# The order of the chosen-key attention, the recurrence's heads and two branches in a two-block layer on one core

## The chip, the core and the metric

The program runs on one core of a Trainium2 chip, in one launch. The metric is the device time of that core in microseconds (us). Three runs of the kernel before gave 1706.37 us as the median, from 1705.73 to 1706.66.

## What is computed

The program is a first block (a convolution branch, a gated linear attention, a hierarchical mixture of experts) and behind it a second block over the same T = 256 tokens of width 1024. The change lies in the second block alone. There u is the normed input and every token gets four branch outputs of width 256: the recurrence (index 0), a pool mixer (1), an attention over chosen keys (2) and an attention into 256 memory tokens (3). Cut to what matters:

```python
z = u @ w_in[l]
(hq, hf, hi, hg, pz, sq, sk, sv, iq, ik, iw, mq) = jnp.split(z, split_pts, axis=-1)
y_a = hgrn2_mixer(hq, hf, hi, hg, lb_all[l], hgrn_norm[l])
y_b = pool_mixer(pz, pool_w[l], pool_scale[l])
y_c = dsa_mixer(sq, sk, sv, iq, ik, iw)
y_m = mem_attention(mq, mk, mv)
merged = None
for bi, y in enumerate((y_a, y_b, y_c, y_m)):
    term = jax.nn.sigmoid(u @ w_gate[l, bi]) * (y @ w_branch[l, bi])
    merged = term if merged is None else merged + term
h = h + rms_norm(merged @ w_out[l], norm_mix_post[l])
u = rms_norm(h, norm_ffn_pre[l])
gt, up = jnp.split(u @ w_ffn_gate_up[l], 2, axis=-1)
h = h + rms_norm((jax.nn.silu(gt) * up) @ w_ffn_down[l], norm_ffn_post[l])
```

The sum over the branches may be taken in any order, so the four branches may follow each other in any order, as long as the weights come in the same one.

## The kernel before, in words

All matrices are fp32. A weight arrives by DMA on SP's queue in pieces of 128x2048 (1 MB, `Stream.load`, L139) and is split in two (`Split.weights`): a high half that ACT copies out (L170), and a low half, raw minus high, whose first 1280 columns DVE computes (L172) and whose other 768 POOL does (L173). Activations are split likewise by ACT and DVE (`Split.act`, L178 and L179; `yh`, `yl`, `uh`, `ul`, `mh`, `ml` are such halves). A product is three matmuls on PE (`Split.mm`, L186 to L188). High and low halves have three buffers each, PSUM's bank tag `ps` (the tiles `pst`) has four, the gates' `sg` two.

In the second block the work around the change is this. `recur(h)` (L1226) does one of the recurrence's four heads: exponentials, elementwise levels on DVE and POOL, matmuls with masked copies in between (L1262, L1263), states (L1268 to L1283). Every second head closes with a norm: square (L1289, ACT), a matmul that sums it (L1291), square root (L1293, ACT, with a load of the root's table), reciprocal and two products on DVE (L1294 to L1296), and a split of the result (L178, L179), of which branch 0's product needs both halves. `choose(t)` finds the top 64 keys for one tile of 128 tokens, `chosen(t)` the attention over them: four logits (L1384, PE), bias and scale (L1391) and the maximum (L1393, both DVE), exponentials (L1322, ACT, with its own table), reciprocals and scaling (L1323, L1324, DVE), four transposes (L1326, PE) copied by ACT (L1333), the values' matmuls (L1338), and a split of the output.

`branch(b)` takes one piece of branch weights and four pieces of gate weights: 4 x 48 gate matmuls of `u` and four groups of 12 matmuls of the branch's output. ACT takes the sigmoid of a gate (L1433), DVE multiplies it with the product (L1435 in the first branch, L1437 after), POOL adds it to `merged` (L1438). Behind the branches stand `w_out` (4 pieces, 96 matmuls over `mh`, `ml`), `add_normed` (the norm of its output, from L1470), `normed_split` (the norm ahead of the FFN: L1103, L1105, a diagonal matrix `dg` at L1109, a turned product at L1115, then `uh` and `ul`), and the FFN.

No engine's order is written out by hand here, except around the norm between `w_out` and the FFN, where ACT, DVE and POOL keep the order of the code. Elsewhere a list scheduler sets each engine's order from the order of the calls (L1445 to L1459) and from its own model of durations; then the engines run through those orders as they stand. Moving two calls can so move instructions anywhere between them and the next fixed point. The order of the weights in memory (`stream2`, L1693) has to be that of the calls.

Of the kernel before, what the change touches and what calls it, by code (L numbers as in the profile page):

```python
# [128 lines left out]
class Stream:  # L129
# [20 lines left out]
    def take(self):  # L150
        self.ahead(1)
        return self.ready.pop(0)
# [894 lines left out]
def second(tc, A, k, out):  # L1047
# [9 lines left out]
    def pt(shape=(P, 512)):  # L1057
        return k.ps.tile(list(shape), F32, tag="ps", name="pst", bufs=k.n_ps)

    def mx(shape=(P, 512)):  # L1060
        return k.ps.tile(list(shape), F32, tag="mx", name="mxt", bufs=8 - k.n_ps)

    with ExitStack() as es:
# [254 lines left out]
        def attend(h, lg, nk, scale, nm, pts):  # L1318

            pe = tp.tile([P, T], F32, tag="a1", name="pe", bufs=k.n_a1)  # L1320
            sm = tp.tile([P, 1], F32, name="sm", bufs=4)
            S.activation(pe[:, :nk], lg, AF.Exp, scale=scale, bias=nm, accum_out=sm[:])  # L1322
            V.reciprocal(sm[:], sm[:])  # L1323
            V.tensor_scalar(pe[:, :nk], pe[:, :nk], sm[:], None, op0=OP.mult)  # L1324
            for c in range(nk // P):
                nc.tensor.transpose(pts[c][:, h], pe[:, c * P:(c + 1) * P], ident)  # L1326

        def values(t, nk, pts, src, y):

            pT = []  # L1330
            for c in range(nk // P):
                pT.append(tp.tile([P, 4, P], F32, tag="a2", name="pT", bufs=k.n_a2))
                S.activation(pT[c][:], pts[c][:], AF.Copy)  # L1333
            py = mx((P, 2, P))
            for h in range(4):
                r = slice(64 * (h % 2), 64 * (h % 2) + 64)
                for c in range(nk // P):
                    nc.tensor.matmul(py[r, h // 2], src(c, h), pT[c][:, h], start=c == 0, stop=c == nk // P - 1)  # L1338
            s = slice(t * P, (t + 1) * P)
            sp.act(yh[y][:, :, s], yl[y][:, :, s], py[:])  # L1340
# [37 lines left out]
        def chosen(t):  # L1378
            nk, neg = P * (t + 1), negs[t]
            pl2 = [mx((P, 2, T)) for _ in range(2)]  # L1380
            for j in range(2):
                for i in range(2):
                    r = slice(64 * i, 64 * i + 64)
                    nc.tensor.matmul(pl2[i][:, j, :nk], sqT[r, j, t * P:(t + 1) * P], skT[r, :nk],  # L1384
                                     start=True, stop=True)
            pts = [mx((P, 4, P)) for _ in range(nk // P)]
            for i in range(2):
                lg = tp.tile([P, 2, T], F32, tag="a2", name="lg", bufs=k.n_a2)
                nm = tp.tile([P, 2], F32, name="nm")
                for j in range(2):  # L1390
                    V.scalar_tensor_tensor(lg[:, j, :nk], pl2[i][:, j, :nk], 64.0 ** -0.5, neg[:, :nk],  # L1391
                                           op0=OP.mult, op1=OP.add)
                V.tensor_reduce(nm[:], lg[:, :, :nk], axis=AX.X, op=OP.max, negate=True)  # L1393
                for j in range(2):
                    attend(2 * j + i, lg[:, j, :nk], nk, 1.0, nm[:, j:j + 1], pts)
            values(t, nk, pts, lambda c, h: sv[:, c], 2)
# [19 lines left out]
        def branch(b):  # L1416

            nonlocal merged
            first = merged is None
            if first:  # L1420
                merged = ap.tile([P, NB, T], F32, tag="merged", name="merged")
            bh, bl = sp.weights(take(), 2)
            for half in range(2):
                def gate_in(i, o):
                    if i % 2 == 0:
                        return
                    blk = half * 4 + i - 1
                    p = pt((P, 2, T))
                    for j in range(2):
                        s = slice((blk + j) * P, (blk + j + 1) * P)  # L1430
                        sp.mm(p[:, j], lambda c: (bh[:, c, s], bl[:, c, s]), lambda c: (yh[b][:, c], yl[b][:, c]), 2)
                    sg = tp.tile([P, 2, T], F32, name="sg", bufs=k.n_sg)
                    S.activation(sg[:], dn.banks[i // 2][:], AF.Sigmoid)  # L1433
                    if first:
                        V.tensor_tensor(merged[:, blk:blk + 2], sg[:], p[:], op=OP.mult)  # L1435
                    else:
                        V.tensor_tensor(sg[:], sg[:], p[:], op=OP.mult)  # L1437
                        G.tensor_tensor(merged[:, blk:blk + 2], merged[:, blk:blk + 2], sg[:], op=OP.add)  # L1438

                dn.turned(X, gate_in)  # L1440
# [4 lines left out]
        choose(1)  # L1445
        choose(0)
        recur(0)
        recur(1)
        recur(2)
        recur(3)  # L1450
        chosen(1)
        chosen(0)
        branch(1)
        branch(3)
        post = ap.tile([P, 2, D], F32, tag="ln2", name="post")
        nc.sync.dma_start(post[:], A["rows2"][:, 2 * D:4 * D].rearrange("o (a d) -> o a d", a=2)
                            .to_broadcast([P, 2, D]))
        branch(0)
        branch(2)  # L1459
        gain = ap.tile([P, D], F32, tag="gain", name="gain")  # L1460
        nc.sync.dma_start(gain[:], A["rows2"][:, 5 * D:].to_broadcast([P, D]))

        def add_normed(t, banks, gain, last=False):

            ss = tp.tile([P, 3], F32, name="rss", bufs=4)
            halves = [slice(0, 512), slice(512, 1024)]
            for half, s in enumerate(halves):
                o = banks[half][:]
                junk = tp.tile([P, 512], F32, tag="a2", name="junk", bufs=k.n_a2)
                S.activation(junk[:], o, AF.Square, accum_out=ss[:, half + 1:half + 2])  # L1470
                V.tensor_tensor(o, o, gain[:, s], op=OP.mult)
                yield
            rs = rms_scale(nc, k, ss)
            yield
            for half, s in enumerate(halves):
                o = banks[half][:]
                V.scalar_tensor_tensor(x[:, t, s] if last else o, o, rs, x[:, t, s], op0=OP.mult, op1=OP.add)
            yield
# [18 lines left out]
        with tc.manual_schedule(engines={E.Activation, E.DVE, E.Pool}):  # L1497
# [7 lines left out]
            a, b = [add_normed(t, banks[t], post[:, 0]) for t in range(2)]  # L1505
# [74 lines left out]
        a, b = [add_normed(t, banks[t], post[:, 1], True) for t in range(2)]  # L1580
# [8 lines left out]
def body(tc, A, out):  # L1589
# [6 lines left out]
    with ExitStack() as es:  # L1596
# [24 lines left out]
        with ExitStack() as mid:  # L1621
# [15 lines left out]
            experts(tc, A, k)  # L1637
        k.stream.open([A["s2"][i] for i in range(A["s2"].shape[0])])
        second(tc, A, k, out)


# [31 lines left out]
def stream2(f):  # L1673

    w, gate, br = f["w_in_2"][0], f["w_gate_2"][0], f["w_branch_2"][0]
    gu, dn = f["w_ffn_gate_up_2"][0], f["w_ffn_down_2"][0]
    out = []

    def add(m):
        out.extend(m.reshape(2, 4, P, 512).transpose(0, 2, 1, 3).reshape(2, P, PIECE))  # L1680

    def rows(m):

        out.append(m.reshape(2, P, D).transpose(1, 0, 2).reshape(P, PIECE))

    add(np.concatenate([w[:, 1536:1792], w[:, 1024:1280]], axis=1))
    add(w[:, 512:1024])
    add(np.concatenate([w[:, 2760:3016], w[:, 2688:2752], w[:, 2048:2112], w[:, 2752:2760], w[:, 2112:2176],
                        np.zeros((D, 56), np.float32)], axis=1))
    add(w[:, 2176:2688])  # L1690
    add(w[:, 0:512])
    add(np.concatenate([w[:, 1792:2048], w[:, 1280:1536]], axis=1))
    for b in (1, 3, 0, 2):  # L1693
        rows(br[b])
        for half in range(2):
            add(gate[b][:, half * 512:half * 512 + 512])
    for half in range(2):
        add(f["w_out_2"][0][:, half * 512:half * 512 + 512])
    for i in range(11):
        add(np.concatenate([gu[:, 256 * i:256 * i + 256], gu[:, D_FF + 256 * i:D_FF + 256 * i + 256]], axis=1))  # L1700
        if i:
            rows(dn[256 * i - 256:256 * i])
    rows(dn[2560:])
    m = f["w_mem_kv_2"][0].reshape(2, 4, P, 512).transpose(0, 2, 1, 3).reshape(2, P, PIECE)
    return np.stack(out), m


def layouts(inp):
# [40 lines left out]
    a["s1"], a["x_by8"] = stream1(f), by8(f["x"])  # L1749
    a["wflr"] = f["w_in"][0][:, 5120:5136].reshape(NB, P, 16).transpose(1, 0, 2)  # L1750
    a["s2"], a["wm"] = stream2(f)
    for n in ("w1", "w3", "w2", "mem_2"):
        a[n] = f[n]
# [17 lines left out]
```

## Time and profile before

| | |
|---|---|
| median of three runs | 1706.37 us |
| profiled execution | 1704.52 us |
| its span | 1702.7 us |
| mean granted TensorE clock | 0.956 |
| PE, DVE, ACT, POOL busy in the span | 88%, 32%, 28%, 28% |
| first block | to some 1225 us |
| recurrence, attentions, branches | to some 1480 us |
| w_out, norms, FFN | to the end |

All times in the trace are microseconds from the start of the span. PE's column tells how long matmuls ran, not how fast: the granted clock stands in a column of its own, and a slow stretch looks busy.

### The profile page before, as it was taken

How to read it: one execution, taken by the hardware profiler on the slowest of the kernel's cores; microseconds unless marked ns; L12 is line 12 of the kernel's file. 1: busy time of each engine (PE TensorE's matmuls, PEld its weight loads, DVE VectorE, ACT ScalarE, POOL GpSimd, SP SyncE). 2: the span in 40 equal slices, each digit the busy share in tenths (PEclk: the TensorE clock that was granted, in tenths of full speed). 3: DMA queues.
4: the chain of work that ended last, by engine and by line, in shares of the span. 5: the costliest groups of instructions: out<-in, count | busy, mean ns of one | idle time of the engine just before them, and what ended most of it. 6: DMA issues, size and time to landing. Idle time of an engine off the chain costs nothing.

```text
span 1702.7 us, 23642 instructions
## 1 busy us (share of the span) xinstructions
PE 1500.3 (88%) x9883; PEld 996.1 (59%) x9883; DVE 544.0 (32%) x1032; ACT 469.0 (28%) x640; POOL 484.9 (28%) x332
## 2 busy tenths in 40 slices
PE   8999999986898878787877878887799998999998
PEld 7999995332353323232322323332499997979997
DVE  5888685110200000010000000000464856453333
ACT  6435651101100000000000000000465544563433
POOL 6777832000000000000000000000354454556563
PEclk9999999997989999999998989999899999999999
DMA  7453679999999999999999999999744332534552
GB/s 276 156 180 140 232 308 349 421 425 426 426 426 426 427 426 426 426 426 426 426 426 426 426 427 426 426 426 426 317 174 149 123 125 100 186 144 178 186 185 74
DMA packets 75693, 533.19 MB, mean 313 GB/s; under 512 B 8497, under 2 KB 9009, under 8 KB 11970
## 3 DMA queue, kind: packets, MB, share of 16 engines
q1 hardware_dynamic: 74178, 526.61, 76.2%
q10 hardware_dynamic: 1408, 5.06, 0.8%
q8 instruction: 78, 1.28, 0.3%
q14 instruction: 29, 0.24, 0.0%
HBM read 530.59 MB, written 1.05 MB: 312 GB/s over the span
## 4 chain that ended last, share of the span: by engine, by line
DMA 45%; PE 26%; DVE 3%; ACT 1%; issue 0%; SPq 0%; DVEq 0%; ACTq 0%
DMA w<-in_w_dram 44%; PE pst L188 6%; PE pst L187 6%; PE pst L186 6%; PE mxt L187 2%; PE mxt L186 2%; PE mxt L188 2%; DMA w<-in_wm_dram 1%; PE pst L833 1%; ACT hi L170 1%; DVE lo L172 0%; PE mxt L1262 0%; PE pst L852 0%; PE pst L1115 0%; PE mxt L1231 0%
## 5 line engine op out<-in xcount | busy, mean ns | idle before, releaser
L173 POOL TENSOR_TENSOR lo<-w,hi 128x768 fp32r<-128x768 f32 (+2 forms) x112 | 381.0, 3407 | 354.7 <-ACT hi L170 244.8
L833 PE MATMUL pst<-w,xe 128*32 128x512 f32 x2048 | 351.2, 669 | 89.1 <-DMA w<-in_w_dram 88.1
L833 PEld LDWEIGHTS pst<-w,xe 128*32 128x32 f32 x2048 | 83.3, 120 | 333.2 <-DMA w<-in_w_dram 163.5
L170 ACT ACTIVATE hi<-w 128x2048 fp32r<-128x2048 f32 (+1 forms) x112 | 209.0, 1868 | 213.0 <-PE pst L187 119.0
L878 POOL TENSOR_TENSOR sw<-S,Wt 128x64 f32<-128x64 f32 x128 | 33.5, 294 | 802.2 <-DVE S L888 558.9
L187 PE MATMUL pst<-ul,hi 128*128 128x256 f32 x736 | 208.6, 284 | 0.0
L188 PE MATMUL pst<-uh,lo 128*128 128x256 f32 x736 | 208.0, 283 | 0.4 <-DVE lo L172 0.4
L186 PE MATMUL pst<-uh,hi 128*128 128x256 f32 x736 | 208.1, 283 | 0.0
L845 DVE TENSOR_TENSOR hd<-si,pst 128x128 f32<-128x128 f32 x64 | 18.5, 289 | 560.0 <-ACT si L844 560.0
L852 PE MATMUL pst<-w,hd 128*32 128x512 f32 x1024 | 171.3, 620 | 25.3 <-DVE hd L845 24.1
L172 DVE TENSOR_TENSOR lo<-w,hi 128x1280 fp32r<-128x1280 f32 (+1 forms) x77 | 124.2, 1613 | 152.4 <-ACT hi L170 142.5
L823 PEld LDWEIGHTS pst<-S,x 128*128 128x128 f32 x1024 | 126.1, 200 | 61.8 <-issue 61.7
L836 ACT ACTIVATE hs<-pst 128x512 f32<-128x512 f32 x32 | 19.1, 597 | 454.5 <-PE pst L833 454.5
L188 PEld LDWEIGHTS pst<-uh,lo 128*128 128x128 f32 x736 | 138.3, 188 | 2.4 <-DVE lo L172 0.9
L186 PEld LDWEIGHTS pst<-uh,hi 128*128 128x128 f32 x736 | 138.8, 189 | 1.5 <-ACT il L1206 0.3
L187 PEld LDWEIGHTS pst<-ul,hi 128*128 128x128 f32 x736 | 138.6, 188 | 1.7 <-issue 0.5
L823 PE MATMUL pst<-S,x 128*128 128x64 f32 x1024 | 135.8, 287 | 1.8 <-DVE S L888 1.5
L408 DVE SCALAR_TENSOR_TENSOR mxt<-U,cols,mxt 128x256 f32<-128x256 f32 x232 | 113.1, 488 | 6.9
L186 PE MATMUL pst<-xh,hi 128*128 128x256 f32 x352 | 98.8, 284 | 5.9 <-ACT hi L170 5.9
L188 PE MATMUL pst<-xh,lo 128*128 128x256 f32 x352 | 98.5, 286 | 0.5 <-DVE lo L172 0.5
L187 PE MATMUL pst<-xl,hi 128*128 128x256 f32 x352 | 98.9, 284 | 0.0
L902 PE MATMUL acc<-ys,WT 64*128 64x512 f32 x256 | 80.8, 615 | 16.4 <-DVE ys L860 16.4
(407 smaller groups left out, 1911.9 us busy)
## 6 DMA issues: line engine op xcount, KB each, us to landing
w<-in_w_dram SPq DMA_DIRECT2D x384, 1024.0 KB, 19.6
w<-in_s_dram SPq DMA_DIRECT2D x108, 1024.0 KB, 4.8
w<-in_wm_dram SPq DMA_DIRECT2D x2, 1024.0 KB, 19.6
rows<-in_rows_dram ACTq DMA_DIRECT2D x1, 1572.0 KB
w<-in_s_dram SPq DMA_DIRECT2D x4, 256.0 KB, 6.7
xn<-in_x_by_dram ACTq DMA_DIRECT2D x1, 1024.0 KB, 9.1
mem<-in_mem_dram ACTq DMA_DIRECT2D x1, 1024.0 KB, 11.4
w<-in_rows_dram SPq DMA_DIRECT2D x1, 1024.0 KB, 19.5
```

The lines of the kernel that those rows point to most:

```text
L170: nc.scalar.activation(hi[:, s], raw[:, s], AF.Copy)
L172: nc.vector.tensor_tensor(lo[:, v], raw[:, v], hf[:, v], op=OP.subtract)
L173: nc.gpsimd.tensor_tensor(lo[:, g], raw[:, g], hf[:, g], op=OP.subtract)
L186: mm(out, lh, rh, start=start and c == 0, stop=False, skip_group_check=True)
L187: mm(out, lh, rl, start=False, stop=False, skip_group_check=True)
L188: mm(out, ll, rh, start=False, stop=stop and c == n - 1, skip_group_check=True)
L408: V.scalar_tensor_tensor(cv[:, blk] if j == 30 else acc, U[:, blk, j:j + T], cols[:, cw + j:cw + j + 1], acc, op0=OP.mult, op1=OP.add)
L823: nc.tensor.matmul(pg[:, c], x1[:, t, c * P:(c + 1) * P], Sx[:, t], start=t == 0, stop=t == 1)
L833: nc.tensor.matmul(ph[g:g + 32, :], xe[:, c, e * CAP:(e + 1) * CAP], w[:, c % 4, :], start=c == 0, stop=c == NB - 1)
L852: nc.tensor.matmul(py[g:g + 32, :], hd[:, j, e], w[:, j % 2, half * 512:half * 512 + 512], start=j == 0, stop=j == 3)
L878: G.tensor_tensor(sw[:, t, dup, :m].rearrange("p (e s) -> p e s", e=n), Sx[:, t].rearrange("p (e s) -> p e s", e=n), wts[t], op=OP.mult)
L902: nc.tensor.matmul(acc[t][half][:], wt_, y, start=False, stop=pr == 31, skip_group_check=True)
```

## The change

Two calls, `chosen(1)` and `chosen(0)`, move from behind the recurrence's last head to places behind its first and second. Branch 2 (chosen keys) moves ahead of branch 0 (recurrence), and the weights with it. No arithmetic is added or taken away; ACT has 50 table loads where it had 48 in the whole program.

```diff
@@ -1445,18 +1445,18 @@
         choose(1)
         choose(0)
         recur(0)
+        chosen(1)
         recur(1)
+        chosen(0)
         recur(2)
         recur(3)
-        chosen(1)
-        chosen(0)
         branch(1)
         branch(3)
         post = ap.tile([P, 2, D], F32, tag="ln2", name="post")
         nc.sync.dma_start(post[:], A["rows2"][:, 2 * D:4 * D].rearrange("o (a d) -> o a d", a=2)
                             .to_broadcast([P, 2, D]))
+        branch(2)
         branch(0)
-        branch(2)
         gain = ap.tile([P, D], F32, tag="gain", name="gain")
         nc.sync.dma_start(gain[:], A["rows2"][:, 5 * D:].to_broadcast([P, D]))
 
@@ -1690,7 +1690,7 @@
-    for b in (1, 3, 0, 2):
+    for b in (1, 3, 2, 0):
```

What the scheduler makes of it is seen in three places. PE's order is the same in both kernels up to some 1353 us (the second head's exponentials), and again from the FFN's first tile on.

**First place: PE at the end of the recurrence's last head.** In the kernel before, this is what PE has in a row (`E`, `att`, `vp` and `st` belong to the head, `sq` to its norm, `skT` and `sqT` to `chosen(1)`; `yh_8056` is the norm's result, the input of branch 0):

```order
L1262 MATMUL mxt<-E 128x128 x8
L1268 MATMUL mxt<-vp,kd 128x64
L1262 MATMUL mxt<-E 128x128 x2
L1268 MATMUL mxt<-vp,kd 128x64 x2
L1279 MATMUL mxt<-att,vp 64x128
L1283 MATMUL mxt<-E,st_8063 64x64
L1279 MATMUL mxt<-att,vp 64x128
L1283 MATMUL mxt<-E,st_8063 64x64 x2
L1291 MATMUL mxt<-sq,cb 128x256
L1384 MATMUL mxt<-skT,sqT 128x256 x4
L186 MATMUL pst<-yh_8056,hi 128x256 x2
```

In the changed kernel 53 gate matmuls stand behind that L1291 and ahead of the first matmul that reads `yh_8056`:

```order
L1291 MATMUL mxt<-sq,cb 128x256
L188 MATMUL pst<-uh,lo 128x256
L186 MATMUL pst<-uh,hi 128x256
L187 MATMUL pst<-ul,hi 128x256
L188 MATMUL pst<-uh,lo 128x256
L186 MATMUL pst<-uh,hi 128x256
```

Before, all 192 gate matmuls of branch 0 are done by then, and the product follows the norm at once; now gate matmuls stand in between.

**Second place: PE, DVE and ACT at `chosen(0)`, which now falls together with the norm of the first two heads.** On PE the changed kernel has in a row (`ch`, `lp` are the third head's exponents, `y_8062` the output of the chosen-key attention):

```order
L187 MATMUL pst<-ul,hi 128x256
L188 MATMUL pst<-uh,lo 128x256
L1291 MATMUL mxt<-sq,cb 128x256
L1384 MATMUL mxt<-skT,sqT 128x128 x4
L1326 MATMUL mxt<-ca,pe 128x128 x4
L1338 MATMUL mxt<-pT,sv 64x128 x4
L1231 MATMUL mxt<-ch,lp 128x512 x6
L186 MATMUL pst<-y_8062,hi 128x256 x2
L186 MATMUL pst<-uh,hi 128x256
```

and ACT at the same place:

```order
L1289 ACTIVATE sq<-mxt 128x256
L170 ACTIVATE hi<-w 128x2048
L1433 ACTIVATE sg<-pst 128x512
L1293 ACT_TABLE_LOAD
L1293 ACTIVATE rs<-mxt,eps_rms 128x256
L1322 ACT_TABLE_LOAD
L1322 ACTIVATE pe,sm<-lg,nm 128x128 x4
L178 ACTIVATE yh_8056<-rs 128x256
L1333 ACTIVATE pT<-mxt 128x512
L178 ACTIVATE y_8062<-mxt 128x2x128
```

and DVE:

```order
L1393 TENSOR_REDUCE nm<-lg 128x2
L1294 RECIPROCAL rs<-rs 128x256
L1323 RECIPROCAL sm<-sm 128x1 x4
L1295 SCALAR_TENSOR_TENSOR rs<-mxt,cols_84,rs 128x256
L1324 TENSOR_SCALAR pe<-pe,sm 128x128 x4
```

No gate matmul stands between the logits, the transposes and the values; before, gate matmuls stood between all three.

**Third place: ACT at the norm ahead of the FFN** (L1470 to L1034 are the second token tile's part of `add_normed`, the `hi` are pieces of FFN weights, `uh` the first tile's input of the FFN). Before:

```order
L1470 ACTIVATE junk,rss<-mxt 128x512 x2
L1033 ACTIVATE rss<-rss 128x1
L1034 ACTIVATE rss<-rss,eps_rms 128x1
L170 ACTIVATE hi<-w 128x2048
L178 ACTIVATE uh<-pst 128x4x128
L170 ACTIVATE hi<-w 128x2048
L178 ACTIVATE uh<-pst 128x4x128
L170 ACTIVATE hi<-w 128x2048
```

and in the changed kernel:

```order
L1470 ACTIVATE junk,rss<-mxt 128x512 x2
L1033 ACTIVATE rss<-rss 128x1
L1034 ACTIVATE rss<-rss,eps_rms 128x1
L170 ACTIVATE hi<-w 128x2048 x3
L178 ACTIVATE uh<-pst 128x4x128 x2
```

All three copies of weights now stand ahead of both `uh`; DVE likewise has its L172 ahead of both `ul`, where it stood between them. On PE, the matmul that closes the first tile's second bank of `w_out` is number 85 of 96, where it was number 71.

## Rows read from the trace of the kernel before

**Rows 1.** Busy time by stretches of the second block; columns in the first line.

```profile
core 0: us, PE busy (x) PEld busy (x) DVE busy (x) ACT busy (x) POOL busy (x), PEclk, DMA share, GB/s
...
1404.00:1420.00 16.00, 16.00 (x127) 15.36 (x127) 9.02 (x16) 6.26 (x8) 10.25 (x10) 1.00 0.43 157
1420.00:1436.00 16.00, 9.29 (x54) 7.20 (x53) 11.80 (x28) 7.35 (x15) 3.12 (x1) 0.85 0.28 107
1432.00:1438.00 6.00, 5.18 (x22) 4.89 (x23) 5.10 (x15) 5.06 (x11) 1.32 (x1) 0.50 0.00 0
1480.00:1496.00 16.00, 16.00 (x70) 12.88 (x69) 8.57 (x12) 10.17 (x19) 9.47 (x3) 1.00 0.49 169
1506.00:1510.00 4.00, 3.86 (x10) 3.05 (x11) 3.17 (x7) 3.13 (x7) 1.16 (x1) 0.57 0.92 373
```

**Rows 2.** PE's waits from 1225 us on: total, times, longest (us).

```profile
PE pst L186 <- ACT yh L178: 3.8, 1, 3.8
```

**Rows 3.** Timeline of the norm behind the last head: start, duration, idle before.

```profile
1426.86 0.70 PE L1291 MATMUL mxt<-sq,cb 128*128 128x256 f32 x2 [0.47 <-ACT sq L1289]
...
1428.12 0.47 ACT L1293 ACTIVATE rs<-mxt,eps_rms 128x256 f32<-128x256 f32 x1
1428.63 1.75 DVE L1294 RECIPROCAL rs<-rs 128x256 f32<-128x256 f32 x1 [2.65 <-ACT rs L1293]
1430.49 0.48 DVE L1295 SCALAR_TENSOR_TENSOR rs<-mxt,cols,rs 128x256 f32<-128x256 f32 x1
...
1432.00 0.42 ACT L178 ACTIVATE yh<-rs 128x256 fp32r<-128x256 f32 x1 [3.40 <-DVE rs L1296]
```

**Rows 4.** Timeline of `chosen(0)` in the kernel before.

```profile
1443.32 0.71 PE L1384 MATMUL mxt<-skT,sqT 64*128 64x128 f32 x8
...
1445.50 1.28 ACT L1322 ACT_TABLE_LOAD   x1
1446.79 0.40 ACT L1322 ACTIVATE pe<-lg,nm 128x128 f32<-128x128 f32 x1
1447.32 0.16 DVE L1323 RECIPROCAL sm<-sm 128x1 f32<-128x1 f32 x1 [0.55 <-ACT pe L1322]
1447.51 0.29 DVE L1324 TENSOR_SCALAR pe<-pe,sm 128x128 f32<-128x128 f32 x1
1450.36 0.27 PE L1326 MATMUL mxt<-ca,pe 128*128 128x128 f32 x1
...
1452.12 0.60 ACT L1333 ACTIVATE pT<-mxt 128x512 f32<-128x512 f32 x1 [0.85 <-PE mxt L1326]
```

**Rows 5.** Timeline: a gate's sigmoid, and the low halves of a weight's split.

```profile
1440.55 0.59 ACT L1433 ACTIVATE sg<-pst 128x512 f32<-128x512 f32 x1
...
1443.47 1.52 DVE L172 TENSOR_TENSOR lo<-w,hi 128x1280 fp32r<-128x1280 f32 x1 [1.19 <-ACT hi L170]
1443.59 3.10 POOL L173 TENSOR_TENSOR lo<-w,hi 128x768 fp32r<-128x768 f32 x1
```

**Rows 6.** Timeline of the norm between `w_out` and the FFN.

```profile
1490.40 0.60 ACT L1470 ACTIVATE junk<-mxt 128x512 f32<-128x512 f32 x1 [1.14 <-PE mxt L188]
...
1495.00 0.54 DVE L1109 TENSOR_SCALAR dg<-ca,rss 128x128 f32<-128x128 f32 x1
...
1496.05 1.95 PE L1115 MATMUL pst<-dg,un 128*128 128x128 f32 x16
...
1497.50 1.89 ACT L170 ACTIVATE hi<-w 128x2048 fp32r<-128x2048 f32 x1
1499.30 0.57 ACT L178 ACTIVATE uh<-pst 128x512 fp32r<-128x512 f32 x1
...
1501.77 3.71 DVE L172 TENSOR_TENSOR lo<-w,hi 128x1280 fp32r<-128x1280 f32 x1 [1.17 <-ACT hi L170]
...
1506.14 0.67 PE L188 MATMUL pst<-hi,ul 128*128 128x512 f32 x1 [1.45 <-DVE ul L179]
...
1510.12 1.95 PE L1115 MATMUL pst<-dg,un 128*128 128x128 f32 x16
```

## The prediction, before the changed kernel was run

> **What bounds the kernel now.** I read the second block by stretches first. Between 1404 and 1420 us PE is busy for all of 16.00 us, with 127 matmuls at full clock, 0.126 us each, while the other engines have room [rows 1]. So PE bounds this part: whatever the change does to ACT, DVE or POOL counts only where PE comes to stand, and then through its clock. In the next 16 us PE is busy for 9.29 alone: 6.71 us of idle time. Behind it the granted clock is 0.50, that is 1.2 GHz, where the stretch before had 2.4: 22 matmuls take 5.18 us, 0.235 each [rows 1], which is 22 x (0.235 - 0.126) = 2.4 us lost. PE had run without a gap before it stood. The whole stall is worth 6.7 + 2.4 = 9.1 us, and the longest wait of PE in the second block lies in it, 3.8 us for `yh` [rows 2]. The timeline shows the chain: the sum of squares on PE, the root on ACT, the reciprocal of 1.75 us, two products, `yh` [rows 3]; 1426.86 to 1432.42 is 5.6 us, and no gate matmul was left to run beside it.
>
> **What is gained: the stall behind the last head.** The changed order has 53 gate matmuls between that norm's matmul and the first reader of `yh_8056`. They are 53 x 0.126 = 6.7 us against a chain of 5.6 us, so the chain is hidden. I count the whole 9.1 us as gone; the short waits for the head's masked copies, part of the 6.7 us, come back under "the heads" below.
>
> **What is paid, first: `chosen(0)` beside the first norm.** Here the changed order has no gate matmul between the logits L1384, the transposes, the values and the third head's L1231. So PE follows the softmax's chain, and ACT first does other work. Counted from the moment when PE reaches L1291 (the last gate matmul ahead of it frees the high half's buffer, so ACT's copy starts there): copy 1.89 [rows 6], sigmoid 0.59 [rows 5], root with its table 1.28 + 0.47, table of the exponential 1.28 [rows 3, 4] make 5.5; four exponentials at 0.40 make 7.1; the last reciprocal 0.16 and L1295's 0.48, which stands ahead of the scalings, 7.7; four scalings at 0.29, 8.9 [rows 3, 4]. Behind them come L1296 (no row; taken as L1295, 0.48), `yh` 0.42 and the copy `pT` 0.60, since ACT has `yh` ahead of `pT`: 10.4. DVE's reciprocal of 1.75 runs beside the exponentials. Of the 10.4 us PE works for 0.70 (L1291), 0.36 (four L1384, half of 0.71) and 4 x 0.27 (L1326) [rows 3, 4], 2.1 in all, and stands for 8.3. Between 7 us (the sigmoid and one scaling less) and 10.5 (the copy one piece later) lie the bounds. After a stand of 6.7 us the clock fell [rows 1]; I take the same 2.4 us here, with 0 and twice that as bounds. **A = 8.3 + 2.4 = 10.7, net of the 9.1 gained: +1.6** (bounds -2.1 to +6.2). So the stall is moved, not removed.
>
> The loads of the two tables lie on this chain. In the trace an exponential follows its load of 1.28 us, begun at 1445.50, at 1446.79 [rows 4], so a change of table costs 1.3 us here. The Trainium skill (ScalarE: Activation LUTs, section "What ACT_TABLE_LOAD costs") puts each change at 1283 ns and a drain of about 1380 ns more. By that A would be 2.8 us dearer and the time 1717.2 us; the row shows no such drain, and I go by the row.
>
> **Second: the end of the branches.** Branch 0 is now last and its 48 product matmuls come at once, with nothing else for PE until `merged` is whole. DVE's lo part (1.52) and POOL's (3.10) stand between the last multiplies and adds [rows 5]. I take 0.6 us, bounds 0 and 1.5 (one lo part of DVE): **B = +0.6**.
>
> **Third: the heads.** The third and fourth head run with lo parts between POOL's level products; one such part is 3.10 us [rows 5], and gate matmuls cover most of it. I take a fifth, 0.6, nearer to the lower bound since PE has gates to run there; bounds 0 and 3.1: **C = +0.6**.
>
> **Fourth: the norm ahead of the FFN.** Let T0 be the end of `w_out`'s last matmul, 1496.05 in the trace, where L1115 starts at once [rows 6]. The first tile's second bank was complete 25 matmuls of 0.229 us (16.00 / 70 [rows 1]) before T0, 5.7 us, and the chain from it to `dg` ends at 1495.54, in time. Now it is complete 11 matmuls before T0, 2.5 us, so the same chain comes 3.2 us later: `dg` begins at T0 + 2.15 where it was T0 - 1.05, and ACT, which was done 0.2 earlier, is free at T0 + 1.9. It has then to do the second tile's two squares with their reads (4 x 0.6 and 0.2, 1.5 in sum) and two small steps of 0.3: the first copy of weights begins at T0 + 4.0, where it began at 1497.50 = T0 + 1.45 [rows 6]. So copy, POOL's lo part and DVE's L172, which took 3.71 us and ended at 1505.48 = T0 + 9.4, all move by 2.55, to T0 + 12.0. Three copies of 1.89 and `uh` 0.57 end at T0 + 10.2; `ul`, now behind L172, lets PE's L188 begin 0.66 after it (as 1506.14 does [rows 6]): T0 + 12.65. But it was the 15th of 24 matmuls that waited there before, and now it is the third: 22 x 0.229 = 5.0 us follow, to T0 + 17.7. With the slow clock of before (10 matmuls in 3.86 us at a mean clock of 0.57, 1.57 lost [rows 1]) it is T0 + 19.3 to the second tile's L1115, against 1510.12 - 1496.05 = 14.07 [rows 6]. **D = +5.2**; bounds +1.4 (clock not falling, and L172 at 1.52 instead of 3.71) and +6.8 (twice the slow clock).
>
> **Without cost:** the DMAs (pieces come in the same number and order of sizes; the queue is busy for 0.28 to 0.43 of these stretches [rows 1]), the `gain` load, which now waits for branch 2's products but is needed much later than 15 us behind them, and two more table loads, of which the ones on a chain are counted above.
>
> **Sum.** 1.6 + 0.6 + 0.6 + 5.2 = +8.0. The profiled execution took 1704.52 us (the median of the three runs is 1.85 above), so it would be 1712.5, and as a median 1706.4 + 8.0 = **1714.4 us**.
>
> **The rivals.**
> - *ACT is ahead of PE (faster).* If the weights' copies are done when PE arrives, A loses 1.89 + 0.59 and the stand is 5.8 us, short enough for the clock to stay; the three copies at the norm lie before T0 as well, B, C and D are nil and the 1.57 us of slow clock there go too. Time: 1706.4 + 5.8 - 9.1 - 1.6 = 1701.5 us. It decides when A's stand and clock together fall below 9.1 less what D costs. For it: ACT is busy for less than half of the 16 us before the stall [rows 1]. Against it: the copy at A waits for a buffer that PE's own last gate matmul frees, and the norm's copies stand in ACT's order behind steps that need `w_out`'s end.
> - *The stall is moved and nothing else happens.* A as above, B, C and D hidden but for D's lower bound less the clock: 1706.4 + 1.6 = 1708.0 us. For it: D rests on one engine's order by a chain of ten steps. Against it: each of the steps has a row.
> - *The change does nothing that counts.* The waits of PE sum to the same: 1706.4 us. For it: no work is added.
> - *The slow clock lasts.* Each new stand costs the clock twice as long (A 13.1, D 6.8), B 1.5, C 1.8: 1706.4 + 4.0 + 1.5 + 1.8 + 6.8 = 1720.5 us. For it: the stand in A is longer than the one that cost 2.4.
>
> **How the numbers follow.** 0.2% of the time, about what a measurement can tell from no change, is 3.4 us: below 1703.0 is faster, above 1709.8 slower. The forecast, 1709.8 to 1719, gets 0.56; ACT ahead 0.10; only moved 0.16; nothing 0.05; lasting clock 0.13. So faster 0.10, same 0.16 + 0.05 = 0.21, slower 0.56 + 0.13 = 0.69. The range leaves out ACT ahead and the upper part of the lasting clock: 1705.5 to 1720.0. The forecast's own range is 1709.8 to 1719.
>
> **What would show it.** In the changed kernel: no wait over 1 us for `yh_8056` behind the last head; a stand of PE of some 8 us at `chosen(0)`, its last releaser ACT's `pT`, with a granted clock of about half behind it; at the norm `dg` late by 2 us or more, `ul` late by more than it was, and some 19 us from `w_out`'s end to the second L1115. I am wrong if PE's stand at `chosen(0)` is below 5 us, if the slow clock there lasts for much longer or not at all, or if those 14 us stay as they are.

## The result, and the profile after

The changed kernel took 1717.68 us (median of 4 runs, 1717.43 to 1719.58), the kernel before 1706.28 (4 runs, 1705.73 to 1706.66). The ratio is 1.0071, with a 95% interval of 1.0059 to 1.0083: the change makes the kernel slower by 11.4 us. The forecast was 1714.4 us in a range of 1705.5 to 1720.0, with 0.69 on slower. The profiled execution took 1717.76 us with a span of 1716.0.

The difference is in one stretch. From the second block's first L1115, at 1228.17 us, to the L1115 of its FFN's second tile, at 1523.39 us, the changed kernel takes 295.22 us, where the kernel before took 282.90 (1227.22 to 1510.12): +12.3 us. Ahead of it the two differ by 0.95 us, and behind it by nothing: 192.61 us here (to 1716.0), 192.58 there. The first view is that of windows, of the changed kernel (columns as in [rows 1]):

```profile
1400.40:1416.00 15.60, 8.00 (x44) 6.18 (x43) 10.36 (x24) 10.18 (x19) 3.58 (x4) 0.67 0.27 100
1416.00:1440.00 24.00, 24.00 (x189) 22.79 (x188) 12.59 (x24) 8.57 (x9) 9.74 (x13) 1.00 0.13 45
...
1503.90:1523.39 19.49, 11.99 (x42) 9.38 (x42) 12.18 (x17) 13.26 (x24) 7.55 (x2) 0.74 0.45 162
```

Two rows are bad. At `chosen(0)` PE is busy for 8.00 of 15.60 us at a mean clock of 0.67; at the norm ahead of the FFN for 11.99 of 19.49 at 0.74. Right behind the first of them PE has its upper clock and no gap for 24 us. The stretch behind the old last head, 9.29 busy of 16 at 0.85 in [rows 1], has no counterpart any more. PE's waits of the second block say the same (engine, what PE ran <- what it waited for: sum us, count, longest):

```profile
PE mxt L1326 <- DVE pe L1324: 6.9, 1, 6.9
PE pst L1115 <- DVE dg L1109: 4.7, 2, 2.5
PE pst L186 <- ACT uh L178: 3.6, 1, 3.6
PE pst L186 <- ACT sg L1433: 2.1, 2, 1.5
PE pst L188 <- DVE lo L172: 1.8, 3, 0.8
...
PE pst L186 <- ACT yh L178: 0.4, 1, 0.4
```

The wait of 3.8 us for `yh` [rows 2] has become 0.4. In its place stands one of 6.9 us for the softmax's scaling.

**The stand at `chosen(0)`.** The timeline of the changed kernel (start, busy us, engine, line; in brackets the wait and what ended it):

```profile
1400.56 1.91 ACT L170 ACTIVATE hi<-w 128x2048 fp32r<-128x2048 f32 x1 [2.14 <-PE pst L187]
1402.54 1.80 POOL L173 TENSOR_TENSOR lo<-w,hi 128x768 fp32r<-128x768 f32 x1 [4.95 <-ACT hi L170]
1402.82 2.87 DVE L172 TENSOR_TENSOR lo<-w,hi 128x1280 fp32r<-128x1280 f32 x1
...
1404.26 0.47 ACT L1293 ACTIVATE rs<-mxt,eps_rms 128x256 f32<-128x256 f32 x1
1404.76 1.28 ACT L1322 ACT_TABLE_LOAD   x1
1405.94 1.74 DVE L1294 RECIPROCAL rs<-rs 128x256 f32<-128x256 f32 x1
1406.05 0.40 ACT L1322 ACTIVATE pe<-lg,nm 128x128 f32<-128x128 f32 x1
...
1407.81 0.47 DVE L1295 SCALAR_TENSOR_TENSOR rs<-mxt,cols,rs 128x256 f32<-128x256 f32 x1
1408.19 0.87 DVE L1324 TENSOR_SCALAR pe<-pe,sm 128x128 f32<-128x128 f32 x4
1408.53 1.12 PE L1326 MATMUL mxt<-ca,pe 128*128 128x128 f32 x4 [6.86 <-DVE pe L1324]
...
1410.39 1.12 PE L1338 MATMUL mxt<-pT,sv 128*64 128x128 f32 x8 [0.75 <-ACT pT L1333]
1411.44 2.93 PE L1231 MATMUL mxt<-ch,lp 128*128 128x512 f32 x6
```

On ACT the chain is the one of the prediction: the copy, the root behind its table, the exponential behind its own, and at the end `pT`, with L1295 ahead of the scalings on DVE. The prediction has only ACT on the chain up to the exponentials, but DVE was as long here: L172, the maximum and the reciprocal L1294 end at 1407.68, the last exponential with its read at 1407.70. By this trace, shortening one of the two alone would not have shortened the stand. PE stands for 6.86 + 0.75 = 7.6 us. Behind it six L1231 in a row take 2.93 us; the fourth head's six in a row, at full clock, take 1.66 in either kernel. The second table load begins at 1404.76 and the exponential at 1406.05, 1.29 us later, so no drain beyond the load shows here either. The 1717.2 us that the prediction gives with such a drain lie closest to the median by chance.

**The norm ahead of the FFN**, in the timeline of the changed kernel:

```profile
1506.13 0.29 DVE L1109 TENSOR_SCALAR dg<-ca,rss 128x128 f32<-128x128 f32 x1
1506.56 3.44 PE L1115 MATMUL pst<-dg,un 128*128 128x128 f32 x16 [2.49 <-DVE dg L1109]
1507.61 5.49 ACT L170 ACTIVATE hi<-w 128x2048 fp32r<-128x2048 f32 x3
...
1511.39 4.11 DVE L172 TENSOR_TENSOR lo<-w,hi 128x1280 fp32r<-128x1280 f32 x1 [3.49 <-ACT hi L170]
1513.01 1.06 ACT L178 ACTIVATE uh<-pst 128x512 fp32r<-128x512 f32 x2
...
1515.43 1.28 DVE L179 TENSOR_TENSOR ul<-pst,uh 128x512 fp32r<-128x512 f32 x2
1516.16 0.80 PE L188 MATMUL pst<-hi,ul 128*128 128x512 f32 x1 [1.37 <-DVE ul L179]
1523.39 1.95 PE L1115 MATMUL pst<-dg,un 128*128 128x128 f32 x16
```

T0, the end of `w_out`'s last matmul, is 1503.9. `dg` begins at T0 + 2.2 (it was T0 - 1.05), all three copies stand ahead of `uh`, `ul` comes behind L172, and the second L1115 follows at T0 + 19.5. In [rows 6] that distance is 14.07.

### The profile page after: what moved, and what is told of

The parts are those of the page before. It is cut to its first block, busy times and chain, and to the rows that moved or that the text cites. A ratio compares the mean times of both kernels' runs of the same rounds, so it can differ in the third digit from the quotient of the medians.

```text
span 1716.0 us, 23639 instructions
## 1 busy us (share of the span) xinstructions
PE 1503.1 (88%) x9883; PEld 997.7 (58%) x9883; DVE 551.2 (32%) x1032; ACT 471.5 (27%) x642; POOL 480.1 (28%) x332
## 3 DMA queue, kind: packets, MB, share of 16 engines
HBM read 530.59 MB, written 1.05 MB: 310 GB/s over the span
## 4 chain that ended last, share of the span: by engine, by line
DMA 41%; PE 29%; DVE 3%; ACT 2%; issue 1%; POOL 0%; SPq 0%; DVEq 0%; ACTq 0%; POOLq 0%
DMA w<-in_w_dram 40%; PE pst L188 5%; PE pst L186 5%; PE pst L187 5%; PE pst L833 2%; PE pst L852 2%; PE mxt L186 2%; PE mxt L187 2%; PE mxt L188 2%; PE pst L823 1%; DVE lo L172 1%; DMA w<-in_s_dram 0%; ACT hi L170 0%; PE mxt L1231 0%; PE pst L1115 0%
## 5 line engine op out<-in xcount | busy, mean ns | idle before, releaser
L173 POOL TENSOR_TENSOR lo<-w,hi 128x768 fp32r<-128x768 f32 (+2 forms) x112 | 375.7, 3360 | 364.1 <-ACT hi L170 333.0
L188 PE MATMUL pst<-uh,lo 128*128 128x256 f32 x736 | 208.5, 285 | 1.8 <-DVE lo L172 1.8
L172 DVE TENSOR_TENSOR lo<-w,hi 128x1280 fp32r<-128x1280 f32 (+1 forms) x77 | 129.7, 1685 | 140.6 <-ACT hi L170 138.8
L188 PEld LDWEIGHTS pst<-uh,lo 128*128 128x128 f32 x736 | 138.3, 188 | 4.5 <-DVE lo L172 2.7
L188 PE MATMUL pst<-xh,lo 128*128 128x256 f32 x352 | 98.6, 287 | 0.6 <-DVE lo L172 0.6
## 6 DMA issues: line engine op xcount, KB each, us to landing
w<-in_wm_dram SPq DMA_DIRECT2D x2, 1024.0 KB, 19.5
```

Source lines behind the costliest of these rows:

```text
L172: nc.vector.tensor_tensor(lo[:, v], raw[:, v], hf[:, v], op=OP.subtract)
L173: nc.gpsimd.tensor_tensor(lo[:, g], raw[:, g], hf[:, g], op=OP.subtract)
L188: mm(out, ll, rh, start=False, stop=stop and c == n - 1, skip_group_check=True)
```

## The experiments

Each kernel was compared with the kernel before on the same chip. Beside the ratio I give the time from the first L1115 to the second (282.90 us before, 295.22 changed), and "D", from T0 to the second L1115 (14.07 and 19.49). The edits are shown against the changed kernel.

**e1, the calls moved alone**, with the branches and the weights as they were:

```diff
-        branch(2)
         branch(0)
+        branch(2)
...
-    for b in (1, 3, 2, 0):
+    for b in (1, 3, 0, 2):
```

> Only the two attention calls are moved; branches and weights stay in the order 1, 3, 0, 2. My theory (the time is PE's stands, and the norm's order is a by-product of what stands ahead of it): the gate matmuls of branches 1 and 3 are used up by the third head, so the last two heads run with nothing beside them, some 10 us of standing each in place of the 6.7 us of before; 24 matmuls stand in the softmax's gap, so that stand falls from 7.6 to about 5; and from w_out's end to the second L1115 it is 14 us as before, not 19.5. Sum about 1722 us (1715 to 1732). Rival (moving the calls is what costs, through the longer softmax chain and the norm, and the branch order is harmless): the same 19.5 us at the norm, and the changed kernel's 1717.7.

Measured: 1722.19 us, ratio 1.0092 (1.0075 to 1.0109); 298.69 us from L1115 to L1115; D 13.4. PE's waits in e1:

```profile
PE mxt L1326 <- DVE pe L1324: 6.9, 1, 6.9
PE pst L186 <- ACT yh L178: 4.1, 2, 3.8
```

The early softmax brings the same stand of 6.9 us, and branch 0 ahead of branch 2 leaves the 3.8 us for `yh` bare. So the stand is paid by the moved calls, and the gain comes from the moved branch. D is not there. The time came out as expected, but not its parts: the stand was to fall to about 5 us and did not, and between 1413 and 1480 us, where the last two heads lie, PE stands for 9.1 us, not for some 10 in each head.

**e2, the branch and the weights moved alone**:

```diff
         recur(0)
-        chosen(1)
         recur(1)
-        chosen(0)
         recur(2)
         recur(3)
+        chosen(1)
+        chosen(0)
```

> Only branches and weights are reordered (1, 3, 2, 0); the calls stay as before. My theory: the chosen-key attention is needed first but comes last, so heads three and four and both softmaxes run with no gate matmul beside them: stands of PE of 25 us and more behind 1400 us; the norm ahead of the FFN as before (14 us). About 1733 us (1722 to 1745). Rival (the two edits add up from parts of their own, and the order of branches is what costs the 5 us at the norm): the norm takes 19.5 us here, and the time is about 1712.

Measured: 1721.93 us, ratio 1.0096 (1.0079 to 1.0113), just below the range that was expected; 299.52 us; D 14.07. PE waits 7.4 us in two pieces at L1326 for the softmaxes' reciprocals. With branch 2 ahead, both softmaxes behind the last head are bare. The expected stands of 25 us and more were too many: between 1400 and 1480 us PE stands for 15.0. Each edit alone costs more than both together, by 3.5 and 4.3 us from L1115 to L1115 (the intervals of the ratios overlap a little): the moved branch 2 needs the calls early, the moved calls need branch 0 late. D is in neither. `w_out`'s order on PE goes with it: the matmul that closes the first tile's second bank is number 71 of 96 in e1 and e2, as before, and number 85 in the changed kernel, e3 and e5. In e7 to e11, which have both edits with the calls at other heads, it is number 71 again and D is gone, so that order is what counts and not the two edits as such.

**e3, `chosen(1)` one head later**, so that both softmaxes stand together behind the second head:

```diff
         recur(0)
-        chosen(1)
         recur(1)
+        chosen(1)
         chosen(0)
```

> As the changed kernel, but chosen(1) and chosen(0) both stand behind the second head: the norm of the first two heads has 78 gate matmuls beside it and no longer lies on the softmax's chain; everything from the third head on, the norm ahead of the FFN too, is as in the changed kernel. My theory (weight copy, sigmoid, root and its table stand ahead of the softmax on ACT): PE's stand at chosen(0) falls from 7.6 us to about 4, and some of the slow clock goes: 1713 us (1710.5 to 1715). Rival (the stand is the softmax's own chain, whatever is beside it): 1717.7 as the changed kernel.

Measured: 1718.32 us, ratio 1.0069 (1.0052 to 1.0085); 295.35 us; D 19.7. The expectation missed; the time is the one of its rival. PE's waits at the softmaxes in e3, and a window of e3 beside the same one of the changed kernel:

```profile
PE mxt L1326 <- DVE sm L1323: 2.9, 1, 2.9
PE mxt L1338 <- ACT pT L1333: 2.4, 2, 1.6
```

```profile
1400.00:1440.00 40.00, 34.69 (x239) 30.65 (x240) 18.90 (x44) 16.39 (x28) 13.63 (x15) 0.87 0.23 80
```

```profile
1400.00:1440.00 40.00, 32.40 (x233) 29.37 (x233) 22.95 (x47) 18.75 (x28) 13.31 (x16) 0.87 0.20 70
```

With 0.6 more for `pe` the waits fall from 7.6 to 5.9 us, and PE is busy for 2.3 us more, yet with 6 matmuls more only, and at the same mean clock of 0.87. What was won in standing went into matmuls that took longer; why the clock gave nothing back there was not tried.

**e4, PE's order at the norm written by hand**, with L1115 drawn ahead of `w_out`'s end and `uh` ahead of the last steps:

```diff
-        with tc.manual_schedule(engines={E.Activation, E.DVE, E.Pool}):
+        with tc.manual_schedule(engines={E.Activation, E.DVE, E.Pool, E.PE}):
...
-            go(na, na, na)
+            go(na, na)
+            up_w.append(sp.weights(take(), 4, cut=0))
             unit(1, 1, 0)
+            go(na)
             unit(1, 1, 1)
-            go(b, b, b)
-            up_w.append(sp.weights(take(), 4, cut=0))
-            go(na, na, b)
+            go(na, na)
+            go(b, b, b, b)
```

> The changed kernel with the order at the norm between w_out and the FFN written out for PE too: the first tile's L1115 stands 12 matmuls ahead of w_out's end, its uh and ul ahead of the second tile's squares. My theory (the 19.5 us from w_out's end to the second L1115 are order alone): at most 10 us instead of 19.5, of which 2 us of L1115 move ahead of w_out's end: 1709.5 us (1706 to 1712). Rival (the time comes back behind, since the FFN waits for its weights' split or loads): 1717.7, within 1.5 us.

Measured: 1721.03 us, ratio 1.0083 (1.0066 to 1.01); 297.60 us. A miss, by an order that made its own waits. PE waits 1.5 and 2.4 us for `mh` and `ml` near the start of `w_out`, 2.0 us for `dg` ahead of the first L1115 and 3.5 ahead of the second. POOL's lo parts and DVE's `dg` in e4's timeline:

```profile
1507.46 9.08 POOL L173 TENSOR_TENSOR lo<-w,hi 128x2048 fp32r<-128x2048 f32 x2 [6.02 <-PE mxt L188]
1509.29 2.85 DVE L1109 TENSOR_SCALAR dg<-ca,rss 128x128 f32<-128x128 f32 x1
```

It settles nothing about D, beyond a warning: a `dg` of 0.29 us took 2.85 beside POOL's lo parts.

**e5, the order of ACT and DVE at the norm.** One call is moved, so that the next weights are asked for ahead of `ups`; by that the scheduler places `uh` and `ul` ahead of two of the three copies:

```diff
             go(na, na, b)
+            w1 = [sp.weights(take(), 4)]
             ups = dn.by_tile(Xt, up_w, up_banks)
...
-            dn.turned(X, gu)
+            dn.turned(X, gu, w=w1 if i == 1 else None)
```

> The changed kernel with one call more at the norm ahead of the FFN: the first weights of the next step are split behind the first tile's uh and ul, so that one copy of weights stands ahead of uh on ACT, not three, and DVE's L172 behind both ul. PE's order is the same. My theory (a good part of the 19.5 us from w_out's end to the second L1115 is ACT's and DVE's order): uh some 3.7 us sooner, L188 no longer behind L172, the second L1115 at 14 to 16 us after w_out's end, 1713.2 us (1711 to 1715.5). Rival (dg's lateness and the lo part on POOL end last, whatever ACT's order is): 18.5 us or more there, 1717.

Measured: 1712.70 us, ratio 1.0037 (1.0024 to 1.0051) against 1706.21; 289.39 us; D 13.6. The timeline of e5 there:

```profile
1507.25 3.40 PE L1115 MATMUL pst<-dg,un 128*128 128x128 f32 x16 [2.50 <-DVE dg L1109]
1510.10 1.19 ACT L178 ACTIVATE uh<-pst 128x512 fp32r<-128x512 f32 x2
1510.71 1.30 DVE L179 TENSOR_TENSOR ul<-pst,uh 128x512 fp32r<-128x512 f32 x2 [2.12 <-ACT uh L178]
1511.18 3.71 ACT L170 ACTIVATE hi<-w 128x2048 fp32r<-128x2048 f32 x2
1518.21 2.02 PE L1115 MATMUL pst<-dg,un 128*128 128x128 f32 x16 [0.40 <-DVE dg L1109]
```

T0 is 1504.6 here. D falls from 19.5 to 13.6 us and the median by 5.0, while `dg` is as late as in the changed kernel (2.50 against 2.49). So `uh` and `ul` behind the copies are worth 5.9 us in this kernel. That is not yet a share of the 5.4 us that D adds, since the same call also shortens the kernel before, as e6 shows.

**e6, the same call moved in the kernel before** (the edit of e5 alone, on that kernel):

> The same one call in the kernel before, whose ACT has one copy ahead of the first uh and one between the two. My theory: the wait of 1.45 us for ul behind L172 goes, and with it some of the slow clock; from w_out's end to the second L1115 12 to 13 us instead of 14.07: 1704.5 us (1702.5 to 1706). Rival (POOL's lo part, for which PE waits 0.7 us there, ends as late as ul did): 1706, no difference.

Measured: 1703.91 us over 11 runs against 1706.21 over 27, ratio 0.9987 (0.9978 to 0.9996); 280.23 us; D 11.4. It is the one version that beats both kernels, by 2.3 us against the kernel before. At the place where 10 matmuls ran at a clock of 0.57 [rows 1], e6 keeps the full clock:

```profile
1505.00:1507.00 2.00, 1.60 (x8) 1.00 (x6) 1.78 (x5) 1.96 (x3) 1.73 (x1) 1.00 0.80 328
```

The timeline of e6, where the first L1115 begins at T0:

```profile
1495.58 1.95 PE L1115 MATMUL pst<-dg,un 128*128 128x128 f32 x16
...
1498.83 1.06 ACT L178 ACTIVATE uh<-pst 128x512 fp32r<-128x512 f32 x2
...
1506.96 2.02 PE L1115 MATMUL pst<-dg,un 128*128 128x128 f32 x16 [0.40 <-DVE dg L1109]
```

With the call in both kernels D is 11.4 here and 13.6 in e5. So 2.2 of the 5.4 us stay: `w_out`'s bank closes later, `dg` and ACT's steps behind it come later, and `uh` begins at T0 + 5.5 in e5 where it begins at T0 + 3.2 here. The other 3.2 us come from the copies ahead of `uh` and `ul`.

**e7, `chosen(0)` one head earlier**, so that no norm stands in its ACT order:

```diff
         chosen(1)
-        recur(1)
         chosen(0)
+        recur(1)
         recur(2)
```

> As the changed kernel, but chosen(0) stands right behind chosen(1), behind the first head: 90 gate and product matmuls lie between its logits, transposes and values. The gates are used up by the last head then, whose norm is bare as in the kernel before. My theory: no stand at chosen(0), 6 to 9 us of stand and slow clock back behind the last head, the norm ahead of the FFN at about 14 us (in w_out's order the first tile's second bank is number 71 again): 1706.5 us (1704 to 1710). Rival (branch 0's 42 products bare ahead of w_out, with merged late on POOL, cost as much as they do in the changed kernel, and more): 1712.

Measured: 1710.05 us, ratio 1.0023 (1.0014 to 1.0033), 0.05 above the expected range; 286.37 us; D 13.8. PE's waits, and three windows of e7:

```profile
PE pst L186 <- ACT yh L178: 3.8, 1, 3.8
```

```profile
1460.00:1464.00 4.00, 2.13 (x12) 1.54 (x11) 3.40 (x6) 1.65 (x1) 2.27 (x1) 0.91 0.47 199
1464.00:1466.00 2.00, 1.95 (x12) 1.64 (x11) 0.58 (x3) 0.01 (x1) 0.84 (x1) 0.50 0.22 33
1474.00:1476.00 2.00, 2.00 (x12) 2.00 (x11) 0.92 (x2) 0.00 (x0) 1.17 (x1) 0.50 0.00 0
```

The stand of 7.6 us at `chosen(0)` is down to 0.2, as the theory says. The run takes the norm out of the chain and puts 90 matmuls into it at once, so it does not tell how much each does. The gates that now cover the softmax are missing behind the last head, where the 3.8 us for `yh` are back (to 1471.49), and the clock is 0.50 from 1464 to 1476.

**e8, e7 with the call of e5:**

> The run before with the one call at the norm: by my theory 1.5 to 2 us less than that run, about 1704.7 us (1702.5 to 1708), below both kernels only if the end of the branches costs nothing new. Rival: no difference from the run before.

Measured: 1707.36 us, ratio 1.0007 (0.9998 to 1.0016); 284.07 us; D 11.4. The call is worth 2.7 us here, 2.3 in e6 and 5.0 in e5, where D had been longest.

**e9, the first two heads' norm behind `chosen(0)`:** the norm's lines are split off `recur` as `close(b)`.

```diff
-        recur(1)
-        chosen(0)
+        recur(1, late=True)
+        chosen(0); close(0)
```

> The changed kernel with the norm of the first two heads split off from the second head and called behind chosen(0): weight copy, root and its table no longer stand ahead of the softmax on ACT, and 26 gate matmuls lie between its logits and transposes. My theory (the stand of 6.9 us was the norm and the copy on ACT, plus the missing gates): stand at chosen(0) at most 3 us. But the gates are one stock: only 5 of them are left behind the last head's norm, where the changed kernel has 53, so 4 to 6 us of stand and some slow clock come back there; the norm ahead of the FFN at 14 us, since w_out's order has the bank at number 71. Time 1709 us (1706 to 1712). Rival (gates are plenty, and a stand removed stays removed): 1703.

Measured: 1711.94 us, ratio 1.0034 (1.0022 to 1.0045) against 1706.43; 289.63 us; D 13.4. The time is at the upper edge of what was expected, though not the waits. PE's waits in e9:

```profile
PE pst L186 <- ACT yh L178: 5.9, 1, 5.9
PE mxt L1338 <- ACT pT L1333: 3.6, 1, 3.6
PE mxt L1326 <- DVE pe L1324: 1.1, 1, 1.1
```

The stand at `chosen(0)` falls to 4.7 us, not below 3: ACT now has a weight copy (from 1402.29), a table load and a sigmoid ahead of `pT`, which begins at 1405.99. And the last head's norm is bare for 5.9: 5 gate matmuls are left to run beside it, where the changed kernel had 53.

**e10 and e11** spread the softmaxes over other heads, with the late norm and the call of e5. The heads' order is r0, r1 late, c1, c0 with the norm, r2, r3 in e10, and r0, c1, r1 late, r2, c0 with the norm, r3 in e11.

> Both attention calls behind the second head, the first norm behind them, and the one call at the norm ahead of the FFN (weights of the next step behind uh): every step of both softmaxes but the last has gates beside it, and the last head's norm is nearly bare. My theory: as e9, less 2.5 us at the FFN's norm: 1706 us (1703 to 1709). Rival (stands are what costs, wherever they lie, and this has the fewest): 1702.

> chosen(1) behind the first head, chosen(0) and the first norm behind the third, with the one call at the norm ahead of the FFN: the third head's levels and chosen(0) are bare, the last head and its norm have gates and to spare. My theory: the stand moves to the third head, 9 to 12 us with its slow clock there, none behind the last head; FFN's norm 11.5 us: 1707 us (1703 to 1712). Rival: the stand behind the last head is what counts, and without it the time is below 1702.

Measured: e10 1716.44 us, ratio 1.0052 (1.0035 to 1.0069), a miss; e11 1709.71, ratio 1.0020 (1.001 to 1.0029), inside its range. The range expected of e10 was 1703 to 1709. Both stands are there, 6.3 us in two pieces for the scalings at L1326 and 5.9 for `yh`: moving the norm took the cover away and left the stand. In e11 none is left behind the last head, and PE stands instead between 1400 and 1420 us, where it is busy for 14.87 of 20 us. None of the orders that put the softmaxes among the heads (the changed kernel, e1, e3, e5, e7 to e11) was faster than the kernel before; e8 cannot be told from it.

## Why the prediction was right, and where it was off

The sign and the places were right. The size was short: the median lies 3.3 us above the forecast, though inside its own range of 1709.8 to 1719. By terms:

| term | said, us | measured, us |
|---|---|---|
| stall behind the last head | 9.1 gained | 9.0 gained |
| A, stand at `chosen(0)` | 8.3 + 2.4 = 10.7 | 7.6 + 2.5 = 10.1 |
| B, end of the branches | 0.6 (0 to 1.5) | 1.9 (0.4 of it for `yh`) |
| C, the heads | 0.6 (0 to 3.1) | 2.4 |
| D, norm ahead of the FFN | 5.2 | 5.4 |
| not foreseen | 0 | 1.5 |
| sum | 8.0 | 12.3 |

- **A held.** The bare PE and the size are as said, and e1 shows that the moved calls bring it; e7, with `chosen(0)` off the norm and gates in between, has 0.2 us of it left. Of the two chains of equal length that end there the prediction names ACT's alone, and no run parts them. The clock behind the stand, 2.5 us, is an estimate from matmuls of one kind at either clock (six L1231 2.93 against 1.66).
- **D held, and the larger part of its cause is shown.** The prediction put `dg`'s start at T0 + 2.15 (2.2 seen), L172's end at T0 + 12.0 (11.6), PE's L188 behind `ul` at T0 + 12.65 (12.3) and the end at T0 + 19.3 (19.5). It has two reasons for that: everything moves by 2.55 us with the late `dg` and ACT behind it, and `ul` behind the copies is now waited for at the third matmul. e5 and e6 together give 2.2 us to the first and 3.2 to the second; the 2.2 are what is left over, as no run takes the late `dg` away by itself. That D is in neither edit alone (e1, e2) was not foreseen; the prediction read it off the final order.
- **B was too small, by a path that it left out.** "I take 0.6 us, bounds 0 and 1.5 (one lo part of DVE)": it took a lo part between the last multiplies and adds. The lo part was there, but PE met it through a buffer:

```profile
1476.61 1.48 DVE L172 TENSOR_TENSOR lo<-w,hi 128x1280 fp32r<-128x1280 f32 x1
1476.77 2.46 POOL L1438 TENSOR_TENSOR merged<-merged,sg 128x512 f32<-128x512 f32 x1 [3.25 <-DVE sg L1437]
1479.26 0.60 ACT L1433 ACTIVATE sg<-pst 128x512 f32<-128x512 f32 x1 [1.90 <-POOL merged L1438]
1479.91 0.39 PE L186 MATMUL pst<-yh,hi 128*128 128x256 f32 x1 [1.47 <-ACT sg L1433]
```

  In this timeline of the changed kernel PE waits for the sigmoid that frees its bank, the sigmoid for a free `sg`, and that for POOL's add, which takes 2.46 us beside DVE's L172 and some 1.3 alone. So some 1.2 of the 1.47 us would be the lo part's, by an estimate from these rows, and the rest that of the two `sg`. The 0.4 us for `yh` were not foreseen: behind the last head the norm's chain took 7.3 us and not 5.6 (L1291 at 1466.95, `yh` done at 1474.26, with a lo part between on DVE), so the 53 matmuls did not cover it whole. This reading is from the trace; no run tries it.
- **C was mis-sized.** That "gate matmuls cover most of it" was too hopeful: waits of 0.60 (`sg`), 0.77 (`lo`) and 0.57 (`att`) between 1416 and 1463 us, and 0.5 more ahead of 1400, sum to 2.4 us, inside the bounds but four times the choice.
- **The last 1.5 us**, what is left of 12.3, are no stands: PE's recorded idle time rises by 8.6 us, and the terms above hold all of it. They lie in steps between gate matmuls that are a little longer than most; no single row carries them, and what makes them stays open.
- **The rivals.** "Only moved" (1708.0) falls, because D is real. "ACT ahead" falls by the stand of 7.6 us, and "nothing that counts" (1706.4) by the time itself. "The clock lasts" (1720.5) priced A at 13.1 and D at 6.8; neither came, though the total came halfway to it by B, C and the small gaps.

## What to carry to other kernels

Matmuls that need nothing are one stock of cover: before a latency chain is moved under them, count which chain loses them, because here every order that was run moved the stand to another place and none removed it. Where a scheduler sets the order, read what a moved call does far downstream: 5.4 of the 12.3 us arose at a norm some 100 us behind the moved calls, 3.2 of them by ACT's order of copies, and one call there was worth 5.0 us in the changed kernel and 2.3 in the one before. Put the small copy on which the matmuls wait ahead of the large copies that are only needed later.

## What the runs showed of the hardware that was not expected

**The clock during a stand and behind it.** Windows of the changed kernel around the stand at `chosen(0)`:

```profile
1405.00:1408.50 3.50, 0.00 (x0) 0.00 (x0) 3.50 (x10) 2.69 (x9) 0.00 (x0) 0.50 0.47 140
1412.00:1414.00 2.00, 2.00 (x6) 1.58 (x5) 0.40 (x1) 1.04 (x2) 0.00 (x0) 0.50 0.00 0
1414.00:1416.00 2.00, 2.00 (x15) 1.90 (x15) 1.82 (x4) 0.75 (x2) 1.77 (x3) 0.81 0.00 0
```

The clock is at its lower level, 1.2 GHz, while PE still stands. It is still there from 1412 to 1414 us, though PE has worked again since 1408.53, and rises in the window behind. In e7 (its windows above) it had fallen by 1464 us, with two short stands of 0.42 and 1.40 us in a stretch that had PE busy for 2.13 of 4 us, and so ahead of the long wait for `yh`; from 1474 to 1476, behind the end of that wait, it is still 0.50. So the clock's price does not follow from the length of one stand. The prediction's 2.4 us was taken from one stand of 6.7 us, and that it fitted the stand in A is in part luck.

**VectorE and GpSimd side by side.** DVE and POOL each compute a part of a piece's low half. In these rows the part that began first took its short time, and the other was stretched. In [rows 5] L172 began 0.12 us ahead of L173: they took 1.52 and 3.10 us. At `chosen(0)` in the changed kernel L173 began 0.28 us ahead: it took 1.80, and L172 took 2.87. At the norm ahead of the FFN L172 began with an L173 under way and took 4.11. POOL's L1438 took 2.46 us in place of some 1.3: it began at 1476.77 inside DVE's L172, and its end at 1479.23 is 1.14 us behind L172's at 1478.09, as if it had worked only from there. That agrees with the Trainium skill (SBUF — State Buffer, "Who interferes with whom"), by which the port pair that the two engines share is an exclusive lock. Which of the two starts first is thus worth more than 1 us to a chain that runs through either of them.
